# Where the low part of a rounded weight tile lies: 4,096 bytes behind its high part where weights are the moving operand, 4,224 where they are stationary

## The chip, the cores and the metric

The kernel runs on one core of one Trainium2 chip. The time is the device time of one execution in microseconds (us); the number compared is the median of several executions of the same program. The engines are named as in the profile: PE is TensorE's matrix multiplication, PEld the loading of its stationary operand, DVE is VectorE, ACT is ScalarE, POOL is GpSimd, SP is SyncE, which here only issues DMAs.

## The reference

One encoder block over 256 tokens with 2,048 channels, in float32. Cut to its matrix products:

```python
hn = rmsnorm(h, mix_norm_pre);  proj = hn @ w_in          # z 1024, xbc 1536, dt 32, u 1024
y_ssd = ssd_mixer(z, xbc, dt, ...)                        # bidirectional SSD scan in chunks of 128
y_pool = pool_mixer(u, pool_w, pool_scale)
h = h + rmsnorm(concat(y_ssd, y_pool) @ w_out, mix_norm_post)
hn = rmsnorm(h, ffn_norm_pre)
gate, val = split(hn @ w_ffn_up)                          # 2 x 5632
h = h + rmsnorm((gelu(dwconv(gate)) * val) @ w_ffn_down, ffn_norm_post)
gate = sigmoid(rmsnorm(h, ple_norm_pre) @ w_ple_gate)
h = h + rmsnorm(gate * (p @ w_ple), ple_norm_post)
```

## The kernel before

**Products in three parts.** Every factor of a large product is held as two tiles of the type that the program calls `F32R`: a high part, the value rounded, and a low part, the rest. `split` (lines 182 to 197) makes them for weights: ACT copies the loaded float32 columns into the high part (line 195), DVE subtracts the high part from the loaded columns and writes the low part (line 196). A product x w is then three matmuls into the same PSUM bank: high x with high w, high x with low w, low x with high w. In this document hh, hl and lh stand for these three.

**Where the two parts lie.** `weight_pair` (lines 178 to 180) takes one of five buffers of 2,112 columns of 4 bytes in each partition, 8,448 bytes; the high part begins at column 0, the low part at column 1,056, that is 4,224 bytes behind it. Most splits use 1,024 or 512 columns of each half; the first stage's tiles (names `dtu0` to `dtu15`) use all 1,056. Three units of the gate product don't take such a buffer: their two parts were given two separate pages of 8,192 bytes (line 1550 for `gtfh` and `gtfl`, line 1619 for `gth` and `gtl`), so there the two parts lie a whole number of 8,192 bytes apart.

**Which operand is which.** A matmul loads its stationary operand (128 columns) and then streams its moving operand (up to 512 columns) past it. All go through `mm` (line 122), so the profile shows all under L123 and they are told apart by tile names.

- Weights stationary, activations moving: the xbc stage (names `xb...`) and the feed-forward up-projection (names `ug...` and `uv...`), both in `feature_pairs` (line 405).
- Weights moving, activations stationary: `dtu...` (the first stage), `z...`, `wo...` (output projection), `dn...` (down-projection), `gt...` (gate) and `ple...`.

**Two kinds of units where weights move.** The contraction runs in units of two 128-row blocks. An ordinary unit has 24 matmuls: two blocks, two token halves, two column halves, three parts. In most ordinary units the column halves alternate innermost, so PE runs hh hh hl hl lh lh (`units`, line 1098, and `token_major`, line 365); in the unit behind a run of fast ones and in the last one the three parts follow each other, hh hl lh. A fast unit (`seven_products`, line 312, and `products`, line 1073) replaces eight block products by seven, at the cost of sums made on DVE or stored ahead; its 21 matmuls run hh hl lh seven times. Counted from the lists of units: z has 8 ordinary units; the output projection 6 ordinary and 2 fast in its first half, 4 and 4 in its second; the down-projection 3 ordinary and 19 fast, then 6 and 16; the gate 5 and 3 in each half, of which three ordinary ones use separate pages; `ple` one ordinary unit in each half. Together that is 36 ordinary units with weights from `weight_pair`, 864 matmuls, and 47 fast units, 987 matmuls.

**Order.** In the mixer and up-projection stages ACT, DVE and SP follow an order written out by hand (`in_order`); PE's order, and all of the rest, is fixed when the program is built. Weights are loaded by SP into three `raw` buffers, split into the five buffers above, and read by PE. A split of a new unit can begin when PE has left a buffer, and a load when DVE has left a `raw` buffer.

Of the kernel before, what the change touches and what calls it, by code (L numbers as in the profile page):

```python
# [86 lines left out]
def build(nc, a, out):  # L87
# [6 lines left out]
    with tile.TileContext(nc) as tc, \  # L94
# [82 lines left out]

        def weight_pair(name):
            w = wp.tile([P, 2112], F32R, tag="w", bufs=5, name=f"{name}w")
            return w[:, :1056], w[:, 1056:]  # L180

        def split(name, src, nel, cuts=()):

            if name in ready:
                return ready.pop(name)
            if name in spare:
                hi, lo = spare.pop(name)
            else:
                hi, lo = weight_pair(name)
            for c0, c1 in zip((0, *cuts), (*cuts, nel)):  # L190
                s = slice(c0, c1)
                v = src[:, s] if name != "dtu0" else r0[:, W_0[c0 // 352]:W_0[c0 // 352] + 352]
                if (name, c0) == ("dtu0", 0):
                    continue
                last["act"] = ins(nc.scalar.copy(hi[:, s], v))
                last["dve"] = ins(nc.vector.tensor_sub(lo[:, s], v, hi[:, s].bitcast(F32)))
            return hi, lo
# [279 lines left out]
        def first_panel(t):  # L477
            c = (V_SCW, W_0[1] - P)[t]
            return put([v[:, t * P:(t + 1) * P] for v in hn(0)], r0[:, c:c + P], r0[:, V_MIX:V_MIX + 1])

        spare["dtu0"] = weight_pair("dtu0")
        turned = ins(nc.vector.tensor_copy(spare["dtu0"][0][:, :352], r0[:, W_0[0]:W_0[0] + 352]))
        with tc.issue_after(turned):
# [870 lines left out]
        for i, w_ in enumerate(which[2:] + which[:2]):  # L1354
            fetch, add, store = block_sums(*w_, i >= len(which) - 2)
            n = 45 * i // 10 + 4
# [379 lines left out]
```

## Time and profile before

| | us |
|---|---|
| median of 3 runs | 1101.53 |
| lowest, highest | 1101.36, 1102.15 |
| the profiled execution's own time | 1101.12 |
| its span, first to last instruction | 1099.3 |

The span is 1.8 us shorter than the time of the same execution; the profiled execution is 0.4 us below the median. TensorE's granted clock over the span is 0.999.

To read it: a matmul's shown duration (394 ns on average for 512 columns) is longer than the distance between the starts of two that follow each other, because they are pipelined. So PE's busy time says little; what counts is the distance from start to start, its pace. It is read from the chain of work that ended last, which gives stretches of PE with their length and their number of matmuls, and from the list of instructions in order of time.

### The profile page before, as it was taken

The numbers are of one execution on the slowest core, as the hardware profiler recorded it, in microseconds if no ns is written. First come the engines' busy times: TensorE is split into PE (matmuls) and PEld (weight loads), VectorE is DVE, ScalarE is ACT, GpSimd is POOL, SyncE is SP. The second block draws the span as 40 slices with busy tenths as digits, with TensorE's granted clock in tenths as the row PEclk, the third lists the DMA queues.
The fourth block names the chain that finished last, engine by engine and source line by source line (L and its number), as shares of the span: only waits on it lengthen the run. The fifth ranks groups of instructions, "written<-read, shape, count | busy, mean of one in ns | idle before, by whom it ended". The sixth has DMA issues, their size and how long they took to land.

```text
span 1099.3 us, 15720 instructions
## 1 busy us (share of the span) xinstructions
PE 1093.2 (99%) x5766; PEld 936.8 (85%) x5766; DVE 976.7 (89%) x1367; ACT 738.3 (67%) x1109; POOL 98.8 (9%) x163
## 2 busy tenths in 40 slices
PE   9999999999999999999999999999999999999998
PEld 9988888888888888888888888888888888888886
DVE  6679988999879888889889988888999999999997
ACT  6687777566775565565756646657688878776773
POOL 0211101100100000000000000000000000051001
PEclk9999999999999999999999999999999999999999
DMA  9987699587589999999999998999999999995872
GB/s 361 423 253 208 193 273 277 211 323 267 186 343 402 395 403 368 393 360 364 385 370 379 366 391 346 401 364 421 356 411 382 370 350 385 418 380 226 312 276 77
DMA packets 59565, 367.45 MB, mean 334 GB/s; under 512 B 6672, under 2 KB 7696, under 8 KB 24208
## 3 DMA queue, kind: packets, MB, share of 16 engines
q1 hardware_dynamic: 45808, 302.74, 70.4%
q0 software_dynamic: 13536, 63.44, 17.3%
q8 instruction: 45, 0.74, 0.2%
q14 instruction: 32, 0.26, 0.1%
q10 hardware_dynamic: 144, 0.26, 0.1%
HBM read 315.56 MB, written 61.34 MB: 343 GB/s over the span
## 4 chain that ended last, share of the span: by engine, by line
PE 97%; DVE 1%; POOL 1%; ACT 0%; issue 0%; POOLq 0%; DVEq 0%; ACTq 0%
PE ga L123 22%; PE va L123 22%; PE dna L123 11%; PE xbc L123 6%; PE woa L123 5%; PE gt L123 5%; PE dns L123 4%; PE dtu L123 4%; PE z L123 4%; PE dn0s L123 2%; PE dn1s L123 2%; PE ple L123 1%; PE wo1s L123 1%; PE gts L123 1%; PE yd L123 1%; PE pw L123 1%
## 5 line engine op out<-in xcount | busy, mean ns | idle before, releaser
L123 PE MATMUL ga<-wox,ug_0w 128*128 128x512 f32 x704 | 130.8, 337 | 0.0
L123 PE MATMUL ga<-wox,ug_1w 128*128 128x512 f32 x704 | 130.1, 337 | 0.0
L123 PE MATMUL va<-wox,uv_1w 128*128 128x512 f32 x704 | 129.2, 337 | 0.0
L123 PE MATMUL va<-wox,uv_0w 128*128 128x512 f32 x704 | 129.2, 337 | 0.0
L123 PEld LDWEIGHTS ga<-wox,ug_0w 128*128 128x128 f32 x704 | 107.6, 188 | 14.5 <-ACT pl L1288 0.2
L123 PEld LDWEIGHTS va<-wox,uv_1w 128*128 128x128 f32 x704 | 107.5, 188 | 14.5
L123 PEld LDWEIGHTS va<-wox,uv_0w 128*128 128x128 f32 x704 | 107.5, 188 | 14.5
L123 PEld LDWEIGHTS ga<-wox,ug_1w 128*128 128x128 f32 x704 | 107.5, 188 | 14.5 <-DVE wox L233 0.2
L304 DVE TENSOR_TENSOR dnb<-dnb 128x512 f32<-128x512 f32 x128 | 88.2, 689 | 3.0
L282 POOL DMA_DIRECT2D dns<-dnb x30 | 16.1, 536 | 317.1 <-DVE dnb L304 266.0
L1205 ACT CAST he<-he 128x512 fp32r<-128x512 f32 x13 | 8.1, 621 | 42.7 <-DVE he L1204 42.7
L123 PE MATMUL xbc<-hn,xb_1w 128*128 128x512 f32 x192 | 36.5, 338 | 0.0
L123 PE MATMUL xbc<-hn,xb_0w 128*128 128x512 f32 (+1 forms) x192 | 36.5, 340 | 0.0
L123 PEld LDWEIGHTS xbc<-hn,xb_0w 128*128 128x128 f32 x192 | 29.7, 188 | 4.1
L123 PEld LDWEIGHTS xbc<-hn,xb_1w 128*128 128x128 f32 x192 | 29.5, 188 | 4.1 <-issue 0.2
L1368 ACT CAST hs<-hid 128x384 fp32r<-128x384 f32 (+1 forms) x44 | 23.4, 537 | 13.6 <-PE dna L123 13.4
L1448 ACT ACTIVATE fc<-gr,vt 128x256 f32<-128x256 f32 x44 | 26.1, 593 | 9.0 <-DVE gr L1441 9.0
L1520 POOL DMA_DIRECT2D hd<-hsum x24 | 12.7, 529 | 193.0 <-PE dn0s L123 70.5
L123 PE MATMUL dna<-dn_0w,hs 128*128 128x512 f32 x108 | 28.6, 394 | 0.0
L123 PE MATMUL dna<-dn_1w,hs 128*128 128x512 f32 x108 | 28.2, 392 | 0.0
L1369 DVE TENSOR_TENSOR hs<-hid,hs 128x384 fp32r<-128x384 f32 (+1 forms) x44 | 25.4, 580 | 2.6 <-ACT hs L1368 2.6
L1451 DVE TENSOR_TENSOR fc<-fc,ft 128x510 f32<-128x510 f32 x22 | 15.1, 689 | 11.3 <-ACT ft L1449 11.3
(1778 smaller groups left out, 2796.8 us busy)
## 6 DMA issues: line engine op xcount, KB each, us to landing
dnb<-w_down SPq DMA_DIRECT2D x32, 1024.0 KB, 10.6
dns<-dnb POOLq DMA_DIRECT2D x30, 1024.0 KB, 7.6
hd<-hsum POOLq DMA_DIRECT2D x24, 512.0 KB, 8.3
dtur<-w_dtu SPq DMA_DIRECT2D x14, 528.0 KB, 9.8
hsum<-he POOLq DMA_DIRECT2D x13, 512.0 KB, 8.0
gtb<-w_gate SPq DMA_DIRECT2D x6, 1024.0 KB, 10.5
gts<-gtb POOLq DMA_DIRECT2D x6, 1024.0 KB, 9.5
dn1r<-w_down SPq DMA_DIRECT2D x6, 1024.0 KB, 7.8
```

The lines of the kernel that those rows point to most:

```text
L123: last["pe"] = ins(nc.tensor.matmul(o, lhsT, rhs, start=start, stop=stop, skip_group_check=True))
L282: nc.gpsimd.dma_start(t, pg[0])
L304: nc.vector.tensor_add(s[:, i], v[:, i], a[:, b])
L1205: nc.scalar.copy(o[:, :512], s[:, :512])
L1368: nc.scalar.copy(t[:, :c1], hid_part(k)[:, :c1])
L1369: nc.vector.tensor_sub(t[:, 512:512 + c1], hid_part(k)[:, :c1], t[:, :c1].bitcast(F32))
L1448: nc.scalar.activation(c[:, f], v[:, f], AF.Identity, bias=vec(V_FCB + 4 * s + 2 * i + f), scale=vec(w + NF))
L1451: nc.vector.tensor_add(c[:, :, 1:], c[:, :, 1:], l[:, :, :L - 1])
L1520: nc.gpsimd.dma_start(o.bitcast(F32), kept[k])
```

## The change

One function is changed. The low part of a pair begins 1,056 columns (4,224 bytes) behind the high part for names that start with `dtu`, `xb` or `u`, as before, and 1,024 columns (4,096 bytes) behind it for all others: `z`, `wo`, `ple`, `dn`, `gt`. The buffer stays as large, the high part stays where it was, and no instruction, load, wait or order is changed.

```diff
         def weight_pair(name):
             w = wp.tile([P, 2112], F32R, tag="w", bufs=5, name=f"{name}w")
-            return w[:, :1056], w[:, 1056:]
+            n = 1056 if name.startswith(("dtu", "xb", "u")) else 1024
+            return w[:, :n], w[:, n:2 * n]
```

## The prediction

> **What bounds the kernel now.** I read the page's first lines and the chain of work that ended last, then busy time by stage.
>
> ```profile
> span 1099.3 us, 15720 instructions
> PE 1093.2 (99%) x5766; PEld 936.8 (85%) x5766; DVE 976.7 (89%) x1367; ACT 738.3 (67%) x1109; POOL 98.8 (9%) x163
> PE 97%; DVE 1%; POOL 1%; ACT 0%; issue 0%; POOLq 0%; DVEq 0%; ACTq 0%
> ```
>
> ```profile
> 136.50:190.80 54.30, 54.30 (x260) 44.32 (x260) 47.59 (x63) 39.84 (x84) 6.88 (x9) 1.00 0.93 279
> 190.80:279.90 89.10, 88.96 (x401) 72.27 (x401) 83.01 (x116) 55.60 (x81) 7.08 (x13) 1.00 0.69 263
> 778.10:997.60 219.50, 219.50 (x955) 178.52 (x954) 210.57 (x251) 172.91 (x221) 27.77 (x28) 1.00 0.95 374
> 1003.60:1086.80 83.20, 83.20 (x383) 68.19 (x382) 77.51 (x109) 58.32 (x85) 5.59 (x13) 1.00 0.62 231
> ```
>
> PE carries 97% of the chain. The four stretches are z, output projection, down-projection and gate, the places where the changed tiles are read (columns: PE, PEld, DVE, ACT, POOL busy, granted clock, DMA share, GB/s). PE has no gap there and the clock is full. So the only thing that could shorten them is a shorter distance between two matmul starts. The second engine is DVE: in the down-projection 210.57 of 219.50 us, 96%, and DMA is at 0.95. These two are what a faster PE would meet.
>
> Next, the pace of PE, from the chain in order of time (start, length, what, number of matmuls).
>
> ```profile
> 263.33 16.59 PE woa L123 x72
> ...
> 334.41 22.19 PE ga L123 x128
> ...
> 818.01 2.06 PE dna L123 x9
> 822.82 2.06 PE dna L123 x9
> ...
> 866.23 2.07 PE dna L123 x9
> 871.08 2.09 PE dna L123 x9
> 875.24 22.14 PE dna L123 x96
> ```
>
> Fast units of the down-projection follow each other at 822.82 - 818.01 = 4.81 us, 21 matmuls, 229.0 ns each. Ordinary units take 16.59/72 = 230.4 and 22.14/96 = 230.6 ns. From 866.23 to 871.08 a fast unit takes 4.85 us, 231.0 ns: some later stretches run a little slower, with no other matmuls in them.
>
> The comparison that carries the argument lies in the same trace: the gate units whose two parts are on separate pages. Their order is hh hl lh as in a fast unit, with 512 columns; the list in order of time:
>
> ```profile
> 1068.35 0.39 PE L123 MATMUL gt<-gth,dnxh 128*128 128x512 f32 x1
> 1068.57 0.39 PE L123 MATMUL gt<-gtl,dnxh 128*128 128x512 f32 x1
> 1068.80 0.39 PE L123 MATMUL gt<-gth,dnxl 128*128 128x512 f32 x1
> ...
> 1071.07 0.69 PE L123 MATMUL gt<-gth,dnxh 128*128 128x512 f32 x2
> ...
> 1085.05 0.28 PE L123 MATMUL gt<-gtl,dnxh 128*128 128x256 f32 x1
> ...
> 1085.65 0.28 PE L123 MATMUL gt<-gth,dnxh 128*128 128x256 f32 x1
> ```
>
> From 1068.35 to 1071.07 there are 12 steps: 2.72/12 = **226.7 ns**. That is 2.3 ns less than the fast units' 229.0, with the same operation, shape and order; the difference is that the low part lies a multiple of 8,192 bytes from the high part instead of 4,224. The five steps of 256 columns from 1085.05 to 1085.65 take 120 ns each. The up-projection agrees: its moving operand is one activation page and never jumps to a low part 4,224 bytes away, and its pairs of one 512 and one 256 take 22.19/64 = 346.7 ns, just 226.7 + 120.0. So 226.7 looks like the undisturbed pace, and the moving operand's jump by 4,224 bytes and back like a disturbance of about 7 ns for three matmuls (687 against 680).
>
> **The change part by part.** It adds and removes no instruction, wait, load or DMA. It does three things.
>
> First, 4,096 in place of 4,224 for moving weights. 4,224 is 128 more than a multiple of 256; 4,096 is one, as 8,192 is, and as the distances between the five buffers (8,448 = 33 x 256) are. The step from the last matmul on one buffer to the first on the next happens seven times in a fast unit, by such multiples of 256, and the unit's loss is already accounted for by the hi-lo-hi jump. I therefore take 4,096 to behave as the separate pages do. No row shows 4,096 itself; the ends are 226.7 ns (free, as the pages) and above today's 229.0 to 230.5 (it costs more than now, the last rival). The term, at the first end:
>
> - fast units: 987 matmuls x (229.0 - 226.7) = 2.3 us;
> - ordinary units: 864 x (230.5 - 226.7) = 3.3 us, less 0.3 because about 8 of the 36 units, those behind a run of fast ones and the last ones, run hh hl lh and lose only 2.3 ns;
> - the slower fast units (4.85 against 4.81): some 9 of them, 0.4 us.
>
> Together 5.7 us, of which the down-projection has 735 x 2.3 + 216 x 3.8 - 0.15 + 0.4, about 2.8.
>
> Second, ACT's and DVE's split. The low part's address moves; would the subtraction change? It reads the high part and writes the low one:
>
> ```profile
> L196 DVE TENSOR_TENSOR dn_0w<-dn1r,dn_0w x6: 1207/1215/1219, 882.7 to 991.3; 128x1024 fp32r<-128x1024 f32 x6
> ...
> L196 DVE TENSOR_TENSOR gtl<-gt1r,gth x4: 1216/1217/1220, 1065.0 to 1073.6; 128x1024 fp32r<-128x1024 f32 x4
> ```
>
> 1215 ns with 4,224, 1217 with separate pages: the distance doesn't show, cost 0.
>
> Third, the stages with stationary weights and the first stage keep 4,224: cost 0.
>
> **What a faster PE meets.** In the down-projection a step that is 1% shorter asks DVE for 210.6 us in about 216.7, 97%.
>
> ```profile
> 801.00:841.00 40.00, 40.00 (x177) 32.75 (x176) 39.00 (x48) 35.52 (x43) 3.17 (x6) 1.00 1.01 416
> 841.00:861.00 20.00, 20.00 (x89) 16.22 (x88) 20.00 (x24) 16.77 (x22) 1.07 (x3) 1.00 0.93 362
> ```
>
> ```profile
> ACT hs L1368 <- PE dna L123: 13.4, 23, 1.7
> ...
> ACT dn122dw L195 <- DMA dn122t<-dns: 1.8, 1, 1.8
> ...
> PEld dna L123 <- DVE dn030dw L196: 0.2, 1, 0.2
> ...
> PEld dna L123 <- DVE dn112dw L196: 0.2, 1, 0.2
> ```
>
> From 801 to 841 DVE has 1.0 us of slack in 8.3 units, 0.12 a unit; a unit is to shrink by 21 x 2.3 = 0.05. ACT waits for PE to leave buffers (13.4 us in 23 waits), so what ACT and DVE do moves forward with PE. But from 841 to 861 DVE is full: unit 15 of the first half makes its four block sums on the spot, and PE is already kept waiting by its split (0.2 us); so also units 6 and 13 of the second half. At these three places DVE sets the pace for about two units; PE's gain of 2 x 0.05 is lost there each time, 0.3 us, and with the waits a little longer I take 0.4 us off. Loads: waits for a DMA are 1.8 us at most, so a few tenths could be lost there as well; taken at nothing.
>
> **Sum:** 5.7 - 0.4, rounded down to 5.2 us for chains outside PE (the 8 us around 200 us, the last 13 us) that don't shrink. The profiled execution's 1101.1 becomes 1095.9; it lies 0.4 below the median, so the median 1101.5 becomes **1096.3 us**.
>
> **The rivals.**
>
> *DVE or DMA takes over the down-projection.* If the 4% of DVE's time that is idle there can't be used, because the loads behind it are late (DMA share 1.01 from 801 to 841), the 2.8 us of that stage are lost: 1101.5 - 2.9 = 1098.6. For it: DVE full for 20 us. Against it: ACT's waits are for PE, hardly ever for a DMA.
>
> *The change does nothing.* The separate pages could be quick for another reason than the distance modulo 256: that PE reads two pages and not one buffer, or only multiples of 8,192 count. Then 1101.5. The Trainium skill speaks for it: "TensorE: Matmul & The Clock Gate", in "Wait — 56ns, not 53.3ns?", gives the distance of warm matmuls as columns over 2.4 GHz plus a fixed 2.5 ns, and "SBUF — State Buffer", in "Who interferes with whom", says that PE never waits on anyone, neither with any term for addresses. By that rule the time stays 1101.5; the trace has 229.0 and 226.7 ns for one shape, both above the page's 215.7, so the rule doesn't hold as it stands.
>
> *4,096 is worse: slower.* Place: PE, at every jump between the parts. The high and low columns of the same number would lie exactly 4,096 bytes apart, and if a memory row repeats at 4,096 each jump could disturb both ways. Price: one more 7 ns for each of the 1851/3 = 617 jumps, 4.2 us: 1105.8. It decides from 5.7/617 = 9.2 ns a jump, today's mean loss. Against it: 8,192 is a multiple of 4,096 and is free, and DVE's subtraction shows no such clash.
>
> **How the numbers follow.** The forecast has 0.66, DVE or DMA 0.13, no effect 0.12, slower 0.09. A difference under 0.2% (2.2 us) can't be told from none. The first two are faster by more (0.79); no effect is within (0.12); the last slower (0.09). Below, the range takes 1094.4: the whole 5.7 and as much as 1.4 more where waits that are now followed by slow stretches settle sooner. Above, 1099.6, past the DVE rival by 1 us; the last two rivals, 0.21, stay out.
>
> **What the profile of the changed kernel would show.** Fast units of the down-projection 4.76 us apart; runs of ordinary units at 226.7 to 227.5 ns (72 in 16.3, 96 in 21.8); the up-projection still 22.19 for 128; the subtraction still 1215 ns; PE waiting for dn030 and dn112 a little longer. The forecast is wrong if the fast units stay at 4.81 (no effect), if they shrink but PE's chain gets stretches of DVE or DMA in the down-projection (the first rival), or if a unit takes over 4.81 with PE unwaited (the last).

## The result, and the profile after

| | before | after |
|---|---|---|
| median (us) | 1102.07, 6 runs (1101.36 to 1102.41) | 1097.76, 6 runs (1096.95 to 1098.02) |
| the profiled execution (us) | 1101.12 | 1097.71 |

The ratio is 0.9961, 95% interval 0.9948 to 0.9973: the change makes the kernel 0.4% faster. The forecast was 1096.3, its range 1094.4 to 1099.6, so the time lies inside it and the sign is right. The gain is smaller than the forecast: 4.3 us between the medians and 3.4 between the two profiled executions, against 5.2.

The first lines of the page of after, and the shares of its chain by engine:

```profile
span 1095.9 us, 15720 instructions
...
PE 1089.0 (99%) x5766; PEld 936.6 (85%) x5766; DVE 976.4 (89%) x1367; ACT 737.8 (67%) x1109; POOL 100.1 (9%) x163
...
PE 91%; DVE 3%; DMA 3%; ACT 1%; issue 1%; POOL 1%; SPq 0%; POOLq 0%; DVEq 0%; ACTq 0%
```

The instructions are the same 15,720, and ACT and DVE are as busy as before within a microsecond. What is new is the chain: before it was 97% PE, now DVE and a DMA have stretches of it.

Where the time went is seen from the starts of the stages, in the chain of work in order of time (start, length, what, number of matmuls). Before:

```profile
136.56 8.32 PE z L123 x35
...
190.80 2.77 PE woa L123 x12
...
279.92 2.80 PE ple L123 x12
...
778.14 5.53 PE dna L123 x24
...
997.66 3.03 PE ple L123 x13
...
1003.74 1.62 PE gt L123 x7
```

After, with some rows between them that are used below:

```profile
136.92 8.25 PE z L123 x35
...
190.52 2.72 PE woa L123 x12
...
262.37 16.33 PE woa L123 x72
278.69 2.80 PE ple L123 x12
...
311.00 22.19 PE va L123 x128
...
776.91 5.46 PE dna L123 x24
...
816.38 2.04 PE dna L123 x9
...
821.14 2.04 PE dna L123 x9
...
849.70 2.34 PE dna L123 x9
...
854.78 2.07 PE dna L123 x9
...
932.89 12.78 DMA dn126r<-w_down
...
994.91 3.03 PE ple L123 x13
...
1000.99 1.60 PE gt L123 x7
```

Subtracting neighbours gives each stage's length:

| stage | before | after | difference |
|---|---|---|---|
| up to z | 136.56 | 136.92 | +0.36 |
| z | 54.24 | 53.60 | -0.64 |
| output projection | 89.12 | 88.17 | -0.95 |
| ple's first half, up-projection | 498.22 | 498.22 | 0.00 |
| down-projection | 219.52 | 218.00 | -1.52 |
| ple's second half to the gate | 6.08 | 6.08 | 0.00 |
| gate to the end | 95.56 | 94.91 | -0.65 |

The gains lie in the four stages whose tiles were moved, and nowhere else: -3.76 us. The 0.36 at the start, where the first loads come in, has nothing to do with the change: a repetition of the same kernel (the last group of experiments) reaches z 0.34 us earlier than this execution.

The pace is what was forecast. Fast units start 821.14 - 816.38 = 4.76 us apart (226.7 ns for each of 21), and 72 matmuls of ordinary units take 16.33 us (226.8 ns, before 230.4). The up-projection's 128 are unchanged at 22.19. DVE's subtraction into the moved low part, in the list of groups with the shortest, the median and the longest duration in ns, is unchanged too (before 1207/1215/1219):

```profile
L197 DVE TENSOR_TENSOR dn_0w<-dn1r,dn_0w x6: 1216/1218/1230, 880.8 to 988.6; 128x1024 fp32r<-128x1024 f32 x6
```

What gave part of the gain back is in the list of waits (who waited, for whom: us in total, times, longest):

```profile
ACT dn126aw L196 <- DMA dn126r<-w_down: 2.0, 1, 2.0
...
PEld dna L123 <- ACT dn126dw L196: 0.8, 1, 0.8
...
PEld dna L123 <- DVE dn030dw L197: 0.4, 1, 0.4
...
PEld dna L123 <- DVE dn112dw L197: 0.3, 1, 0.3
...
PEld dna L123 <- DVE dn030bw L197: 0.2, 1, 0.2
```

Before, PE waited 0.2 us each for dn030 and dn112 and not at all for dn126. These are the three units named in the prediction: unit 15 of the first half, 6 and 13 of the second. The first of them also shows in the chain, where the unit from 849.70 to 854.78 takes 5.08 us instead of 4.76. Summed over the list of all matmuls in the down-projection, counting as wait what each step over 243 ns takes beyond 226.7 ns, the waits grew from 0.3 to 1.4 us, while the other steps shrank by 2.7.

(Line numbers behind the changed function are one higher than before: the split is L196 and L197.)

### The profile page after: what moved, and what is told of

Same layout as the page of the kernel before. It is cut to its first block, busy times and chain, and to the rows that moved or that the text cites. A ratio compares the mean times of both kernels' runs of the same rounds, so it can differ in the third digit from the quotient of the medians.

```text
span 1095.9 us, 15720 instructions
## 1 busy us (share of the span) xinstructions
PE 1089.0 (99%) x5766; PEld 936.6 (85%) x5766; DVE 976.4 (89%) x1367; ACT 737.8 (67%) x1109; POOL 100.1 (9%) x163
## 4 chain that ended last, share of the span: by engine, by line
PE 91%; DVE 3%; DMA 3%; ACT 1%; issue 1%; POOL 1%; SPq 0%; POOLq 0%; DVEq 0%; ACTq 0%
PE ga L123 22%; PE va L123 22%; PE dna L123 8%; PE xbc L123 6%; PE woa L123 5%; PE gt L123 5%; PE z L123 4%; PE dtu L123 4%; PE dns L123 3%; PE dn0s L123 2%; DMA dn126r<-w_down 1%; DMA dn114t<-dns 1%; PE ple L123 1%; PE wo1s L123 1%; PE dn1s L123 1%; PE gts L123 1%
## 5 line engine op out<-in xcount | busy, mean ns | idle before, releaser
L1369 ACT CAST hs<-hid 128x384 fp32r<-128x384 f32 (+1 forms) x44 | 23.5, 538 | 12.3 <-PE dna L123 12.1
```

Of the source, the lines that this page charges most:

```text
L1369: nc.scalar.copy(t[:, :c1], hid_part(k)[:, :c1])
```

## The experiments

"Moving" weights are the ones that stream past the stationary operand. In the compiled program the high parts of all weight tiles and the pages that hold activations begin at byte 96 modulo 256 of a partition; a low part 4,224 bytes behind is at 224, one 4,096 behind at 96.

### Which distances are free: 4,352 and 4,160

```diff
-            n = 1056 if name.startswith(("dtu", "xb", "u")) else 1024
-            return w[:, :n], w[:, n:2 * n]
+            n = 1056 if name.startswith(("dtu", "xb", "u")) else 1088
+            return w[:, :1056 if n == 1056 else 1024], w[:, n:n + (1056 if n == 1056 else 1024)]
```

The second kernel has 1040 in place of 1088, that is 4,160 bytes, 64 more than 4,096.

> Moving weights: low part 4,352 bytes behind the high part (17 x 256, not a multiple of 4,096); the rest as in the changed kernel. Theory 'jump in steps of 256': the pace is that of the changed kernel, 226.7 ns, fast units of the down-projection 4.76 us apart. Rival 'multiples of 4,096': back to the pace before, 4.81 us apart and 230.5 ns in ordinary units.

> Moving weights: low part 4,160 bytes behind the high part (64 more than a multiple of 256). Theory 'jump in steps of 256': it costs, fast units 4.81 us apart or about that. If a finer step is enough (64 bytes), 4.76 us. Under the rival 'multiples of 4,096' it costs too.

Measured: 1097.62 us with 4,352 and 1103.65 with 4,160 (one run each; the kernel before took 1101.48 to 1103.0 in 14 runs beside them). Chain with 4,352:

```profile
262.69 16.33 PE woa L123 x72
...
816.71 2.04 PE dna L123 x9
...
821.47 2.04 PE dna L123 x9
```

Chain with 4,160:

```profile
263.64 16.61 PE woa L123 x72
...
784.76 2.09 PE dna L123 x9
...
789.64 2.09 PE dna L123 x9
```

4,352 is 17 x 256 and neither a multiple of 512 nor of 4,096, and it is as good as 4,096: 4.76 us a fast unit. So a multiple of 256 is enough. 64 off costs more than 128 off: 4.88 us a fast unit, where 4,224 had 4.81.

### Both parts 128 off, with 4,096 between them

```diff
-            n = 1056 if name.startswith(("dtu", "xb", "u")) else 1024
-            return w[:, :n], w[:, n:2 * n]
+            if name.startswith(("dtu", "xb", "u")):
+                return w[:, :1056], w[:, 1056:]
+            return w[:, 32:1056], w[:, 1056:2080]
```

The low part stays where it was before the change; the high part moves to it, modulo 256.

> Moving weights: the low part stays where it was before the change (column 1,056), the high part moves up by 32 columns (128 bytes), so the two are 4,096 bytes apart and both lie 128 bytes off the place of the high part before. Theory 'jump': only the distance counts, fast units 4.76 us apart, time about 1097.8 us. Rival 'place of the low part' (a moving operand at that place is slow by itself, or clashes with the stationary operand there): now all three matmuls are slow, 4.81 us or more, up to 4.90 (21 x 7 ns over 4.76), time 1102 us or more.

Measured: 1105.8 us median (5 runs, 1105.45 to 1105.97), ratio to the kernel before 1.0034 (1.0021 to 1.0047): slower than before. Its chain:

```profile
264.71 16.73 PE woa L123 x72
...
790.87 2.09 PE dna L123 x9
...
795.75 2.09 PE dna L123 x9
```

There is no jump by 4,224 here, the distance is the same 4,096 as in the changed kernel, and each fast unit takes 4.88 us instead of 4.76. So the distance between the parts doesn't by itself make the pace, and the prediction's "jump by 4,224 bytes and back" falls as a mechanism. What is left: the place of the moving operand itself, or its place relative to something else.

### Everything shifted by 128, and the activations alone

```diff
+        cpad = cp.tile([P, 32], F32, name="cpad")
+        nc.gpsimd.memset(cpad, 0.0)
```

That pad stands ahead of all tiles. In the second kernel it stands in the pool of the pages with the activations, so they move by 128 bytes and the weights don't.

```diff
+        wpad = gp.tile([P, 32], F32, tag="gpad", bufs=1, name="gpad")
+        nc.gpsimd.memset(wpad, 0.0)
```

> The changed kernel with 32 unused columns (128 bytes) ahead of everything else, so that weight buffers and activation pages all move up by 128 bytes together. Theory 'place against the other operand' (moving and stationary operand quick when their addresses differ by a multiple of 256): nothing changes, fast units 4.76 us apart, time about 1097.8. Rival 'absolute place' (the place 128 bytes up is slow by itself): as e3, fast units 4.88 us apart, time about 1106.

> The changed kernel with 32 unused columns between the weight buffers and the activation pages, so that only the activations move up by 128 bytes. Theory 'place against the other operand': all moving weights now lie 128 bytes off their stationary operands, as in e3: fast units 4.88 us apart, time about 1106; the up-projection, where high and low part only change roles, stays at 22.19 us. Rival 'absolute place': moving weights stay quick, 4.76 us, and the up-projection, whose moving operand has moved, is slower than 22.19 us.

Measured: 1096.96 us with everything shifted, 1113.41 with the activations alone (one run each; the kernel before took 1100.97 to 1102.17 in 13 runs beside them). Chain with everything shifted:

```profile
310.58 22.19 PE va L123 x128
...
792.16 2.04 PE dna L123 x9
...
796.92 2.04 PE dna L123 x9
```

Chain with the activations alone shifted:

```profile
264.92 16.80 PE woa L123 x72
...
314.20 22.53 PE va L123 x128
...
803.33 2.09 PE dna L123 x9
...
808.21 2.09 PE dna L123 x9
```

Moving both operands together leaves the pace; moving one of them against the other costs as much as in the run with both parts 128 off (4.88). So where weights move, it is the **place of the moving operand relative to the stationary one, modulo 256 bytes**, that makes the difference. It isn't the whole of it, matmul by matmul: with 4,160 only one matmul of three lay off, by 64, and the unit took as long as here with all three off by 128. The expectation that the up-projection would stay at 22.19 missed: it went to 22.53. There the weights are stationary. Before this shift their high part was level with the activations and the low part 128 off; now it is the other way round, and that arrangement is slower.

### 4,096 for stationary weights as well

```diff
-            n = 1056 if name.startswith(("dtu", "xb", "u")) else 1024
+            n = 1056 if name.startswith("dtu") else 1024
```

> 4,096 bytes also where weights are stationary (xbc and up-projection); only the first stage keeps 4,224. Theory 'jump of the moving operand': nothing changes against the changed kernel, the up-projection stays at 22.19 us for 128 matmuls, time about 1097.8 us. Rival 'any two parts that PE reads in turn count, stationary ones too': the up-projection's stretches change from 22.19 us; by 7 ns for each of 64 pairs it would be 22.64 or 21.74, and the 22 such stretches 10 us more or less.

Measured: ten runs in two groups, six at 1096.97 to 1098.68 and four at 1106.29 to 1107.23; ratio to the kernel before 0.9987 (0.9961 to 1.0013), which says little of two groups. The profile is of the upper group (1106.42):

```profile
311.39 22.61 PE va L123 x128
...
801.93 2.04 PE dna L123 x9
...
806.69 2.04 PE dna L123 x9
```

The down-projection has the good pace, 4.76; the whole loss lies in the up-projection, 22.61 - 22.19 = 0.42 us for 128 matmuls, 9.2 us for its 2,816 (four rows of 704 on the page). That is the distance between the groups. With 4,224 the up-projection took 22.19 in every profile in which the activations hadn't been shifted against the weights. So the rule above doesn't carry over to stationary weights: in the profiled run, with both parts level with the moving operand, the up-projection was slower than with the low part 128 off. The two groups suggest that its pace takes one of two values from run to run. No run of the lower group was profiled, so its pace is inferred from the time alone, and what decides between the two was not found. This is why the change's split by names matters.

### No block sums on DVE at the three full places

```diff
-                    t = page(f"{name}t")
-                    add_blocks(r, t)
+                    nc.vector.tensor_copy(page(f"{name}t")[:, :1], r[:, :1])
...
-            if r is t:
+            if r is t and stage not in APART:
```

The four block sums that DVE makes on the spot in each of three units are left out, in the changed kernel and, in the second run, in the kernel before.

> The changed kernel without the four block sums that DVE makes on the spot for three fast units of the down-projection (a copy of one column stands in their place), so the product is not the reference's. Theory 'DVE takes back a part of the gain at these three units': PE's waits at units 15 of the first half and 6 of the second go, the down-projection is 0.6 to 1.1 us shorter than in the changed kernel, time 1096.7 to 1097.2. If DVE has no part in it (only late loads), 0.2 us or less.

> The same left out in the kernel before (4,224 bytes everywhere). PE waited there for DVE by 0.1 us at two places, so 0.1 to 0.3 us shorter than before: about 1101.7. The difference to e7 is then the gain of the change with its cover back, 5.0 us, against 4.3 us measured.

Measured: 1096.53 us with 4,096 (4 runs, 1096.32 to 1097.17; ratio to the kernel before 0.9955, 0.9938 to 0.9972) and 1101.43 with 4,224 (10 runs, 1100.67 to 1102.2; 0.9998, 0.9988 to 1.0007). The change is worth 1101.43 - 1096.53 = 4.9 us here, against 4.3 with the sums (4.7 in the repetition below). PE's waits without the sums, with 4,096:

```profile
PEld dna L123 <- DVE hs L1369: 0.7, 1, 0.7
PEld dna L123 <- DVE dn_0w L197: 0.4, 1, 0.4
```

No wait for dn030, dn112 or dn126 is left, though dn126's load still lands late (12.3 us after its issue; ACT waits 1.2 us for it). Of the 1.4 us of waits in the down-projection, 0.7 are gone. In the medians this is near the scatter; in the traces it is plain: from its first chain row to ple's, the down-projection is 1.0 us shorter without the sums (218.00 to 216.99).

With 4,224 it is 0.6 shorter (219.52 to 218.88), more than the 0.1 to 0.3 expected, and not because of waits. The fast units at 4.85 us, which the prediction noted without a cause, are gone; every fast unit now takes 4.81, as in these rows of the run with 4,224:

```profile
866.52 2.06 PE dna L123 x9
871.33 2.06 PE dna L123 x9
```

With the sums such units stand behind the ones where PE waited for DVE, from 856 and from 922 us on. So a wait seems to leave PE at a slower pace for several units, with the operands where they were; how is open. With 4,096 the pace is back at 4.76 us two units behind the wait (859.57 to 864.33 in the chain of after). In the down-projection the change is thus worth 1.5 us with the sums and 1.9 without.

### The late load, and ple's pace

The first load of the gate (1 MB) is issued right ahead of dn126's. Of the three kernels here the first is the changed kernel again; the second issues that load at unit 15; the third also moves ple's stationary operand, which lay 32 bytes off.

```diff
-  at={13: first_raw,
+  at={15: first_raw,
```

```diff
+        cp.tile([P, 8], F32, name="pad_a")
         pth = cp.tile([P, 2, L], F32R, name="pth")
         ptl = cp.tile([P, 2, L], F32R, name="ptl")
+        cp.tile([P, 56], F32, name="pad_b")
```

> The changed kernel as it is, on the same chip and in the same call as the two that follow, so that differences of half a microsecond can be read. Expected: about 1097.8 us as in its first comparison (1096.95 to 1098.02), 0.4% below the kernel before; in the down-projection PE again waits 0.8 us for dn126dw on ACT, which is behind a load of dn126r that lands 12.8 us after its issue. If that wait is a matter of chance between executions, it is 0.2 or less this time.

> The first raw load of the gate stage (gtf, 1 MB) is issued two units of the down-projection later, at unit 15 instead of unit 13 of the second half, so that it no longer stands ahead of dn126's load. Theory (the load that lands late is what costs PE the 0.8 us at dn126): that wait goes, dn126r lands in about 10 us, and the kernel comes out 0.5 to 1.0 us below the changed kernel of the same call, about 1097.0. Rival (DVE's block sums at that unit are what costs the time, the late load only moves the name of the wait): PE waits as long for dn126's split, now behind DVE, and the time stays at 1097.8. A second rival: the wait moves to a later unit, dn130 or dn132, whose load now stands behind gtf; the time stays at 1097.8 as well.

> As the run before, and the two tiles of the embedding (pth, ptl), the stationary operand of ple's products, are moved by 32 bytes, so that they lie at the same place modulo 256 as the weight tiles that stream past them; everything behind them is moved by 256 bytes in all, so its relations stay. Theory (the place of the moving operand relative to the stationary one sets the pace): ple's 48 matmuls go from 233 to 226.7 ns, 0.3 us less than the run before, about 1096.7. Rival (ple is slow for another reason, the place of PE's output or its neighbours): they stay at 233 ns.

Measured, 5 runs each: 1097.22 us for the changed kernel again (1097.18 to 1098.56; ratio 0.9962, 0.995 to 0.9975), 1097.73 with the later load (1097.32 to 1098.4; 0.9965, 0.9953 to 0.9978), 1097.53 with ple's operand moved as well (1096.77 to 1098.07; 0.9961, 0.9947 to 0.9975). These three are the same within what can be told; no version beats the changed kernel.

Issue to landing of dn126's load, in us in the last column, in the changed kernel run again:

```profile
dn126r<-w_down SPq DMA_DIRECT2D x1, 1024.0 KB, 12.7
```

and with the gate's load later, followed by what PE then waited for:

```profile
dn126r<-w_down SPq DMA_DIRECT2D x1, 1024.0 KB, 10.5
```

```profile
PEld dna L123 <- DVE dn126bw L197: 0.7, 1, 0.7
```

The load comes 2.2 us sooner, ACT's wait for it is gone, and PE still waits at the same unit, now for DVE: 0.7 us, where the changed kernel run again waited 0.6 there. The third kernel, with the same later load, waited 0.4, so a difference of 0.3 is scatter here. So the theory of the late load fell and its first rival held: the load only gave the wait another name. Together with the run without the sums, where the load was late and nothing waited at dn126, DVE's work at that unit is what costs.

ple's pace, with its operand 32 bytes off:

```profile
278.46 2.80 PE ple L123 x12
```

and level:

```profile
278.88 2.73 PE ple L123 x12
```

From 233 to 227.5 ns a matmul: the rule of the relative place foretold it. 48 such matmuls are 0.3 us, too few to be seen in the time.

## Why the prediction was right, and where it wasn't

**Which rows would move, and how far: right.** The pace of the separate pages, 226.7 ns, is that of the moved tiles: 4.76 us a fast unit and 16.33 us for 72, as written down; the up-projection and the subtraction stand still. Summed from start to start over all matmuls of each stage, steps up to 243 ns alone, the pace brought 0.6 (z), 1.1 (output projection), 2.7 (down-projection) and 0.7 (gate): 5.1 us of a term of 5.7.

**The missing part of that term.** ple was counted among the 36 ordinary units, 48 x 3.8 ns = 0.2 us, and gained nothing: it never ran at 230.5 but at 233, and its stationary operand is 32 bytes off the weights' high part whatever the low part does. The rest of the 0.6 lies in z, the down-projection and the gate, 0.1 to 0.2 us each.

**DVE's three places: the right ones, at too small a price.** The step "PE's gain of 2 x 0.05 is lost there each time ... I take 0.4 us off" failed in size. In the down-projection PE's waits grew by 1.1 us, mostly at these three units, and 0.2 more came in the output projection. The runs without the sums show the cause: the waits for these units go. Not all of the 1.1 is theirs: without the sums the change still lengthens the waits from 0.3 to 0.7 us, above all one for `hs` near 880 us (0.4 to 0.7), so about 0.8 belongs to the three places. And the term of 0.4 for the slower fast units hung on the same sums, as the run with 4,224 and no sums shows. Why the loss at one place is more than the gain of two units was not tested; a likely reading is that PE comes to the full place sooner by what it gained over several units ahead of it, and waits until DVE is done. "Waits for DMA taken at nothing" looked wrong in the trace of after, but the run with the later load bears it out.

So the sum stands at 5.1 - 1.3 for the waits = 3.8 from the list of matmuls; the stages, which hold steps of other kinds too, give 3.76, and the start of the profiled execution takes 0.36 of it. The median gained 4.3, and 4.7 in the repetition (1101.89 to 1097.22).

**The reason given for the pace: wrong, though its number was right.** The prediction laid the disturbance to the moving operand's jump between its parts. With no jump but 4,096, and both parts 128 off the stationary operand, the pace was worse than before, and with all tiles shifted alike it stayed good. The losses don't simply add up: with one of three matmuls 128 off (before) a fast unit's matmul loses 229.0 - 226.7 = 2.3 ns on average and an ordinary unit's 3.7, with all three off 4.88 us / 21 - 226.7 = 5.7. So the order of the three parts counts too, and how is open. The jump and the relative place make the same forecast for 4,096, because the high part happens to lie level with the activations: that the forecast came out was luck in this respect, and only these three runs tell the two apart. The agreement that the prediction saw in the up-projection was chance as well: its pairs do take 346.7 ns, but in the list of matmuls before it is 229 ns from the start of a matmul with 512 columns to the next start and 118 from one with 256, not 226.7 and 120.

**The rivals.** "DVE or DMA takes over" happened in part, and its sign came: PE's chain has stretches of DVE and DMA in the down-projection. Waits took back 1.1 of that stage's 2.7 us, and the runs with the later load and without the sums lay the waits at the full places on DVE. "The change does nothing" fell. The Trainium skill, "SBUF — State Buffer", in "Who interferes with whom", counts two read ports of PE, one for the moving operand and one for the weight load, and calls them independent; the traces differ with it, since shifting one of the two against the other took a fast unit from 4.76 to 4.88 us. Which memory or port clashes is not shown by any run here. "4,096 is worse" fell for moving weights; for stationary ones 4,096 was indeed worse in four of ten runs, by 9 us.

## What to carry to other kernels

Where matmuls follow each other without a gap, compare the start-to-start pace of units of the same shape within one trace; two paces for one shape may point to where the operands lie (here a wait ahead could also slow the units behind it), and a few bytes of padding were worth 0.4% here. Where weights move, look at the place of the moving operand relative to the stationary one, modulo 256 bytes, and shift all tiles, one tile and the other tile to tell a distance from a place. Before counting such a gain in full, find the units where another engine is already full: PE arrives there sooner, and waits.

## What the runs showed of the hardware

- Pace of a 512-column matmul with moving weights in this kernel, each with its own load of the stationary operand: 226.7 ns with the operands level modulo 256; 232.4 with the moving one 128 off; 233 with the stationary one 32 off (ple), 227.5 when it was put level. With one part of three 64 off, a fast unit takes 4.88 us, as much as with all three 128 off.
- Up-projection, stationary weights: 22.19 us for 128 matmuls with the high part level and the low part 128 off (every profile with 4,224 there and the activations unshifted); 22.61 us with both parts level, in the one profile taken. Four of that program's ten runs have the time that goes with 22.61; the other six are 9 us shorter and have no profile.
- With the roles of the parts exchanged (the high part 128 off, the low part level) the same 128 take 22.53 us.
- With one matmul of three 128 off, fast units that followed a wait of PE ran at 4.85 us instead of 4.81 for several units; without DVE's sums, and so without that wait, all ran at 4.81.
